# A recurrent scan that steps two head pairs at once

## The chip, the cores and the metric

The kernel runs on one NeuronCore of a Trainium2 chip, in float32 throughout. The metric is the device time of one execution in microseconds (us), taken as the median of several runs. Engines are named as in the profile: PE (TensorE matmul), PEld (its weight loads), DVE (VectorE), ACT (ScalarE), POOL (GpSimd), SP (SyncE, which here only issues DMAs). Each engine takes its instructions in the order in which they were queued.

## The reference

One post-norm layer over 1024 latent tokens with a prefix of 256 context tokens, width 1024. The part that matters here is branch B of the token mixer, a bidirectional RWKV-7 scan with 8 heads of 64 channels:

```python
def delta_scan(state0, inputs, emit):
    def step(S, inp):
        r_t, w_t, k_t, v_t, kk_t, a_t = inp
        s_kk = jnp.einsum('...vk,...k->...v', S, kk_t)
        S = (S * w_t[..., None, :] - s_kk[..., :, None] * (kk_t * a_t)[..., None, :]
             + v_t[..., :, None] * k_t[..., None, :])
        return S, (jnp.einsum('...vk,...k->...v', S, r_t) if emit else None)
    return lax.scan(step, state0, inputs)
...
state_ctx, ys_c = delta_scan(state0, scan_c, ctx_out)   # 256 context tokens, outputs not used
_, ys_l = delta_scan(state_ctx, scan_l, True)           # 1024 latent tokens
```

Around it stand one wide input projection `h @ w_in`, neighbourhood attention (branch A), a chunked gMLP (branch C), the merge of the three branches by gates, and a SwiGLU FFN. Direction 1 of the scan runs over the tokens backwards.

## The kernel before, in words

The program is written as if it ran one stage after the other: projections, scan (`rwkv_run`), 4 projections that only the attention needs, attention with the scan's read-out mixed in, 24 projections that only the merge needs, merge and output projection, FFN. A scheduler then orders the instructions of each engine at build time: what stands earlier in the program has the higher priority, and what is ready and stands later fills the time of an engine that it takes to be idle, as far as tiles and PSUM banks are free. The order is fixed from then on.

The 28 late projections (`filling`, called through `fill`) are the **filler**: each is 48 matmuls of 128 x 128 x 512 (lines 208 to 210, three per product because a float32 is split in a high and a low part), 1344 matmuls in all. They use 2 PSUM banks of their own, tag `d`.

The scan turns the recurrence into products over 64 tokens (a unit). Heads go in pairs: a pair fills 128 partitions. A **job** is one head pair, both directions, and 4 units (256 tokens): 4 pairs x 5 pieces of the sequence = 20 jobs. The list `L` takes the pairs in two groups, and within a group the jobs of its two pairs alternate, so that job m hands its state on to job m+2. For each job there is

- `prep`, per direction: loads of five rows of 256 tokens; exponentials on ACT; products on DVE; the Gram products `ge` and `go` (lines 643, 644) and the transposes `tr` (line 647) into PSUM tiles of tag `gr`; copies from there by DVE (lines 654 to 667, G and others) and ACT (line 670).
- `invert`, for both directions together: the inverse of a unit lower triangular 64 x 64 matrix for each unit and head. G goes out to DRAM (`gs`, line 679) and comes back in another layout (`gz`, line 681); 30 small dependent DVE instructions invert the 16 x 16 diagonal blocks (lines 689 and 691) and one copies the result (line 692); it goes out (`ds`, line 694) and comes back (`Dc`, line 696); `Db` and `Dt` are made of it (line 705); then four rounds of 8 small matmuls each (lines 710 and 719, PSUM tag `ho`), each followed by DVE (lines 712, 722), finish X for one direction, and the same again for the other.
- `step`, for each unit and direction, in the order of the tokens: two products with the state (731, 732), a copy to `ru`, the product with X (736), a negated copy to `ub` by ACT and DVE (740, 741), three products that make the new state and the output (742 to 744), the scaled state (755 by DVE, 756 by ACT) and two copies of the output `y` by ACT (760).

`prepare(m)` (prep and invert) is written two jobs ahead of the steps of job m. Six PSUM banks belong to the scan: three of tag `gr`, one of `ho`, two of `sc` (`ngr` is 3 in line 88). A PSUM tile of a tag waits until one of the tag's banks is free of the tile that had it.

## Time and profile before

| | |
|---|---|
| median of 3 runs | 2478.57 us (2476.95 to 2483.38) |
| the profiled execution | 2475.12 us; its span 2473.3 us |
| granted clock of TensorE | 0.986 on average |
| PE, PEld, DVE, ACT, POOL busy | 96%, 76%, 59%, 33%, 25% of the span |
| scan, from the first Gram product to the last state product | about 517 to 1203 us |
| attention and read-out | about 1203 to 1467 us |
| last filler, then merge, output projection and FFN | 1467 to 1487 us, then to the end |

A row of a group gives how often an instruction ran, its busy time and the mean of one; matmuls are pipelined, so two of them overlap in the records, and the time that one costs PE is read from start to start. Each float32 matmul of the scan is recorded as two passes; a filler matmul is one. A row of the timeline gives start, duration, engine, line and tiles, and in brackets what ended an idle time before it. An SPq or ACTq row is the issue of a DMA on that engine's queue.

### The profile page before, as it was taken

What the parts mean: (1) busy time and instruction counts of PE and PEld (TensorE: products, weight loads), DVE (VectorE), ACT (ScalarE), POOL (GpSimd) and SP (SyncE); (2) the same over time, 40 slices, a digit from 0 to 9 for tenths busy, and PEclk for the clock granted to TensorE, in tenths of its full rate; (3) what the DMA queues carried; (4) which work ended last, traced back from release to release, by engine and by line L of the source; (5) the groups of instructions that cost most, each with busy time, mean ns of one, the idle gap of its engine ahead of it and who ended that gap; (6) DMA issues with size and microseconds to landing.
All of it is one profiled execution on the core that took longest, in us unless ns stands there. A gap on an engine that the chain in (4) does not pass through costs nothing.

```text
span 2473.3 us, 39035 instructions
## 1 busy us (share of the span) xinstructions
PE 2386.2 (96%) x14752; PEld 1879.6 (76%) x14752; DVE 1447.2 (59%) x3318; ACT 819.8 (33%) x1721; POOL 628.3 (25%) x654
## 2 busy tenths in 40 slices
PE   6999999989999999999999999999999999999997
PEld 4778888876777776777777777777778888888886
DVE  8884446357788877887278855685562323232226
ACT  4433334233344433443356632232311121111112
POOL 6220213441112111121132230324522222212224
PEclk9999999999899999999999999999999999999999
DMA  7675434553334433332467656453311111111101
GB/s 253 206 240 159 138 126 164 170 165 78 94 97 108 106 98 94 93 101 62 138 170 204 182 188 233 151 184 118 102 51 52 51 51 43 43 51 47 47 26 69
DMA packets 263840, 293.90 MB, mean 119 GB/s; under 512 B 121666, under 2 KB 192578, under 8 KB 263652
## 3 DMA queue, kind: packets, MB, share of 16 engines
q1 hardware_dynamic: 200852, 213.12, 29.3%
q10 hardware_dynamic: 54608, 51.40, 6.7%
q0 software_dynamic: 8192, 26.88, 2.9%
q8 instruction: 117, 1.92, 0.3%
q14 instruction: 71, 0.58, 0.1%
HBM read 221.06 MB, written 70.26 MB: 118 GB/s over the span
## 4 chain that ended last, share of the span: by engine, by line
PE 65%; DVE 8%; DMA 3%; issue 3%; POOL 2%; ACT 1%; SPq 0%; POOLq 0%; ACTq 0%; DVEq 0%
PE d L209 11%; PE d L208 11%; PE d L210 11%; PE d L1001 3%; PE d L1002 3%; PE d L1000 3%; PE pv L884 2%; PE ho L719 2%; PE gr L644 2%; PE sc L736 2%; PE sc L731 1%; PE gr L643 1%; PE sc L744 1%; PE pt L870 1%; PE sc L742 1%
## 5 line engine op out<-in xcount | busy, mean ns | idle before, releaser
L209 PE MATMUL d<-hl,wh 128*128 128x512 f32 x1584 | 641.6, 405 | 0.4 <-POOL hl L1089 0.4
L208 PE MATMUL d<-hh,wh 128*128 128x512 f32 x1584 | 638.7, 403 | 0.2 <-ACT hh L1086 0.2
L210 PE MATMUL d<-hh,wl 128*128 128x512 f32 x1584 | 636.8, 402 | 0.0
L208 PEld LDWEIGHTS d<-hh,wh 128*128 128x128 f32 x1584 | 299.7, 189 | 64.8 <-issue 1.6
L210 PEld LDWEIGHTS d<-hh,wl 128*128 128x128 f32 x1584 | 299.6, 189 | 64.9 <-issue 2.3
L209 PEld LDWEIGHTS d<-hl,wh 128*128 128x128 f32 x1584 | 299.6, 189 | 61.7 <-POOL hl L1089 1.0
L200 POOL TENSOR_TENSOR wl<-wr,wh 128x256 fp32r<-128x256 f32 (+1 forms) x156 | 192.5, 1257 | 591.2 <-ACT wh L196 536.1
L196 ACT ACTIVATE wh<-wr 128x1024 fp32r<-128x1024 f32 x123 | 130.2, 1059 | 354.3 <-PE d L209 222.7
L1126 DVE TENSOR_TENSOR sl<-sl,d 128x512 f32<-128x512 f32 x44 | 30.2, 687 | 300.9 <-PE d L210 300.9
L200 DVE TENSOR_TENSOR wl<-wr,wh 128x1024 fp32r<-128x1024 f32 x51 | 63.3, 1242 | 160.0 <-ACT wh L196 111.6
L1000 PE MATMUL d<-dwh,S 128*128 128x512 f32 x352 | 137.2, 390 | 2.0 <-DVE acc L1153 2.0
L1001 PE MATMUL d<-dwl,S 128*128 128x512 f32 x352 | 136.9, 389 | 0.0
L1002 PE MATMUL d<-dwh,S 128*128 128x512 f32 x352 | 136.9, 389 | 0.0
L1153 DVE TENSOR_TENSOR acc<-d,acc 128x512 f32<-128x512 f32 x96 | 64.7, 686 | 95.5 <-PE d L1002 95.4
L995 POOL TENSOR_TENSOR dwl<-dr,dwh 128x1024 fp32r<-128x1024 f32 (+1 forms) x24 | 55.5, 2318 | 163.3 <-ACT dwh L994 163.3
L756 ACT ACTIVATE rv<-sc,E 64x64 f32<-64x64 f32 x152 | 46.5, 308 | 139.9 <-DVE rv L755 130.8
L884 PE MATMUL pv<-pT,V 128*64 128x128 f32 (+2 forms) x640 | 92.0, 284 | 0.0
L994 ACT ACTIVATE dwh<-dr 128x1024 fp32r<-128x1024 f32 (+1 forms) x24 | 23.7, 989 | 192.8 <-PE d L1002 185.3
L995 POOL TENSOR_TENSOR wl<-wr,wh 128x1024 fp32r<-128x1024 f32 x16 | 43.7, 2734 | 170.2 <-ACT wh L994 126.5
L225 DVE TENSOR_TENSOR S<-sl,S 128x512 fp32r<-128x512 f32 x44 | 66.2, 1505 | 30.8 <-ACT S L222 30.8
L884 PEld LDWEIGHTS pv<-pT,V 128*64 128x64 f32 (+2 forms) x640 | 69.0, 138 | 16.5 <-issue 11.1
L722 DVE TENSOR_TENSOR X<-ho,Dt 48x192 f32<-48x192 f32 (+2 forms) x240 | 68.3, 285 | 21.5 <-PE ho L719 16.5
(308 smaller groups left out, 4752.8 us busy)
## 6 DMA issues: line engine op xcount, KB each, us to landing
wr<-wgu SPq DMA_DIRECT2D x44, 512.0 KB
wa<-wada SPq DMA_DIRECT2D x32, 512.0 KB
wr<-win SPq DMA_DIRECT2D x31, 512.0 KB
wr<-win ACTq DMA_DIRECT2D x28, 512.0 KB
s_gt<-stg ACTq DMA_DIRECT2D x48, 256.0 KB
wr<-wbr SPq DMA_DIRECT2D x24, 512.0 KB
g<-s_gt SPq DMA_DIRECT2D x48, 256.0 KB
dr<-wdn SPq DMA_DIRECT2D x20, 512.0 KB
```

Of the source, the lines that this page charges most:

```text
L196: nc.scalar.activation(hi[:, :n], raw[:, :n], AF.Copy)
L200: (lo_eng or self.lo_eng).tensor_tensor(lo[:, q], raw[:, q], hi[:, q].bitcast(F32), ALU.subtract)
L208: nc.tensor.matmul(ps, w, xh, start=first and k == 0, stop=False)
L209: nc.tensor.matmul(ps, w, xl, start=False, stop=False)
L210: self.last = nc.tensor.matmul(ps, lo[:, P * k:P * k + P], xh, start=False, stop=last and k == n - 1)
L225: (lo_eng or nc.vector).tensor_tensor(lo, src, hi.bitcast(F32), ALU.subtract)
L722: nc.vector.tensor_tensor(X[z:z + n, :, t0:64], e[z:z + n], Dt[z:z + n, :, t0:64], ALU.add)
L884: nc.tensor.matmul(o, V[0:k, vt, 64 * e:64 * e + 64], pt[0:k, i, :], start=(i == 0), stop=(i == len(cols) - 1))
L995: nc.gpsimd.tensor_tensor(lo[:, 0:512 * n], raw[:, 0:512 * n], hi[:, 0:512 * n].bitcast(F32), ALU.subtract)
L1000: nc.tensor.matmul(ps, xh, wh, start=first, stop=False)
L1001: nc.tensor.matmul(ps, xh, wl, start=False, stop=False)
L1002: nc.tensor.matmul(ps, xl, wh, start=False, stop=last)
```

## The change

A job now holds both head pairs of a group for 128 tokens, 2 units of each pair, so that there are again 20 jobs (2 groups x 10 pieces), with two steps after each other instead of four, and job m hands its state on to job m+1. A step (`step_in`, `step_solve`, `step_out`) takes one unit of both pairs. The copies of a step cover both pairs in one instruction; `ub` and `us` are one form, written by ACT alone; the state is scaled by DVE alone, in one instruction per head. The products of a step stand in two banks, `sa` and `sb` of two buffers each: first and second product in `sa`, state and output in `sb`, there as matmuls of 64 columns, the two column halves one after the other, where before one matmul had 128 columns. That makes 10 matmuls per unit where there were 7 (8 instead of 7 in the context's units). The loads of a job bring two pieces of 128 tokens where they brought one of 256, so there are twice as many DMAs, of half the size; the same holds for the stores of `y`. `gr` has two banks instead of three, and `ho` has none of its own: its tiles are now of tag `gr`.

```diff
@@ -85,7 +85,7 @@
-        self.nd, self.ngr = 2, 3
+        self.nd, self.ngr = 2, 2
...
-            ub = rp.tile([P, P], F32, name=f"ub{i}")
+            ub = rp.tile([P, 2, P], F32, name=f"ub{i}")
             nc.gpsimd.memset(ub, 0.0)
             self.ub.append(ub)
-        L = [(2 * g + j, i) for g in range(2) for i in range(5) for j in range(2)]
+        L = [(g, i) for g in range(2) for i in range(10)]
...
         def values(m):
-            j, i = L[m]
+            g, i = L[m]
             rv = rvs[m] = [[self.T([P, 4, 64], f"rv{d}{h}", 3) for h in range(2)] for d in range(2)]
...
                 for h in range(2):
-                    nc.sync.dma_start(rv[d][h][64 * (1 - h):64 * (1 - h) + 64, 0:4, :],
-                                      bass.AP(V.tensor, V.offset + 64 * h + n0 * P, [[P, 64], [P * 64, 4], [1, 64]]))
+                    for jj in range(2):
+                        V = s["vtok"][2 * g + jj]
+                        nc.sync.dma_start(rv[d][h][64 * (1 - h):64 * (1 - h) + 64, 2 * jj:2 * jj + 2, :],
+                                          bass.AP(V.tensor, V.offset + 64 * h + n0 * P, [[P, 64], [P * 64, 2], [1, 64]]))
...
-        for m, (j, i) in enumerate(L):
+        for m, (g, i) in enumerate(L):
...
-            y = [self.T([P, 2, P], f"y{d}", 2) for d in range(2)] if i else [None, None]
-            for u in range(4):
+            lat = i >= 2
+            y = [self.T([P, 2, P], f"y{d}", 2) for d in range(2)] if lat else [None, None]
+            for uu in range(2):
+                st = [self.step_in(Js[m][d], d, uu, rvs[m][d]) for d in range(2)]
+                ub = [self.step_solve(Js[m][d], *st[d]) for d in range(2)]
                 for d in range(2):
-                    self.step(Js[m][d], d, i, u, rvs[m][d], rvs[m + 2][d] if i < 4 else None, y[d])
-            if i:
+                    self.step_out(Js[m][d], d, uu, ub[d], st[d], rvs[m][d], None if i == 9 else rvs[m + 1][d], y[d])
...
+                    n = i - 2 if d == 0 else 9 - i
+                    for jj in range(2):
+                        nc.scalar.dma_start(s["Y"][d][2 * g + jj][:, P * n:P * n + P], y[d][:, jj, :])
...
     def start(self, d, i):
-        return 0 if i == 0 else (CT + 256 * (i - 1) if d == 0 else NT - 256 * i)
-
-    def prep(self, m, j, d, i):
+        return P * i if d == 0 else (CT - P * (i + 1) if i < 2 else NT - P * (i - 1))
...
-        for t, x in ((li, s["li"][d]), (kk, s["kk"]), (kd, s["kd"][d]), (bb, s["bb"][d])):
-            nc.sync.dma_start(t, x[j][:, n0:n0 + 256])
-        if lat:
-            r = self.T([P, 256], "rl", 2)
-            nc.sync.dma_start(r, s["r"][j][:, n0 - CT:n0 - CT + 256])
+        r = self.T([P, 256], "rl", 2) if lat else None
+        for t, x, n in ((li, s["li"][d], n0), (kk, s["kk"], n0), (kd, s["kd"][d], n0), (bb, s["bb"][d], n0), (r, s["r"], n0 - CT)):
+            for jj in range(2):
+                if t is not None:
+                    nc.sync.dma_start(t[:, P * jj:P * jj + P], x[2 * g + jj][:, n:n + P])
...
         ge = self.ps.tile([P, 4, P], F32, name="gr", tag="gr", bufs=self.ngr)
...
-            e = self.ps.tile([P, 4, 64], F32, name="ho", tag="ho", bufs=1)
+            e = self.ps.tile([P, 4, 64], F32, name="ho", tag="gr", bufs=self.ngr)
...
-                e = self.ps.tile([P, 4, n], F32, name="ho", tag="ho", bufs=1)
+                e = self.ps.tile([P, 4, n], F32, name="ho", tag="gr", bufs=self.ngr)
...
-    def step(self, J, d, i, u, rv, rvn, y):
...
+    def step_in(self, J, d, uu, rv):
         nc = self.nc
+        tt = uu if d == 0 else 1 - uu
+        sa = self.ps.tile([P, 2, 256], F32, name="sa", tag="sa", bufs=2)
+        sb = self.ps.tile([P, 2, 256], F32, name="sb", tag="sb", bufs=2)
+        halves = (slice(0, 64), slice(64, 128))
+        kk = J["KKe"], J["KKo"]
+        for jj in range(2):
+            for z, q in enumerate(halves):
+                nc.tensor.matmul(sa[q, jj, 0:64], kk[z][:, 2 * jj + tt, 0:64], rv[z][:, 2 * jj + tt, :], start=True, stop=True)
+        for jj in range(2):
+            for z in range(2):
+                for h, q in enumerate(halves):
+                    if J["lat"] or h == z:
+                        nc.tensor.matmul(sb[q, jj, 64 * z:64 * z + 64], kk[z][:, 2 * jj + tt, 64 + 64 * h:128 + 64 * h],
+                                         rv[z][:, 2 * jj + tt, :], start=(jj == 0 and (z == 0 or not J["lat"])), stop=False)
+        return tt, sa, sb
+
+    def step_solve(self, J, tt, sa, sb):
+        nc = self.nc
+        ru = self.T([P, 2, 64], "ru", 2)
+        nc.vector.tensor_copy(ru, sa[:, :, 0:64])
+        for jj in range(2):
+            for z in (0, 64):
+                nc.tensor.matmul(sa[z:z + 64, jj, 64:128], J["X"][z:z + 64, 2 * jj + tt, :], ru[z:z + 64, jj, :], start=True, stop=True)
+        self.un += 1
+        ub = self.ub[self.un % 4]
         for z in (0, 64):
+            nc.scalar.activation(ub[z:z + 64, :, z:z + 64], sa[z:z + 64, :, 64:128], AF.Copy, scale=-1.0)
+        return ub
+
+    def step_out(self, J, d, uu, ub, st, rv, rvn, y):
+        nc = self.nc
+        tt, _, sb = st
+        BB, E = J["BB"], J["E"]
+        for jj in range(2):
+            for h in (0, 64):
+                q = slice(h, h + 64)
+                c = slice(0, P) if J["lat"] else q
+                nc.tensor.matmul(sb[q, jj, c], BB[:, 2 * jj + tt, q], ub[:, jj, c], start=False, stop=(jj == 1))
+        if uu == 0 or rvn is not None:
+            n, w = (rv, 1 - tt) if uu == 0 else (rvn, d)
+            for z in range(2):
+                q = slice(64 * z, 64 * z + 64)
+                nc.vector.tensor_tensor(n[z][q, w::2, :], sb[q, :, q], E[q, tt::2, 64:65].to_broadcast([64, 2, 64]), ALU.mult)
+        if J["lat"]:
+            for z, p0 in ((0, 64), (1, 0)):
+                nc.scalar.activation(y[64 * tt:64 * tt + 64, :, 64 * z:64 * z + 64], sb[p0:p0 + 64, :, 64 * z:64 * z + 64], AF.Copy)
```

How this moves instructions on PE, as the built programs have them. First the kernel before, in the middle of the scan. Tiles carry numbers: `ho_7412` belongs to the inversion whose G is `G_7299`, while `gr_8040` to `gr_8095` are the Gram products and transposes of a later job.

```order
L643 MATMUL gr_8040<-KKe4_3962,BK_8035 128x64
L644 MATMUL gr_8041<-KKo4_3963,BK_8035 128x64
...
L647 MATMUL gr_8050<-c_ident_63,BK_8035 128x128 x2
...
L643 MATMUL gr_8085<-KKe5_3966,BK_8080 128x64 x4
L710 MATMUL ho_7412<-Db_7406,G_7299 64x64 x8
L719 MATMUL ho_7423<-Dt_7407,ET_7421 48x48 x8
L719 MATMUL ho_7434<-X_7408,ET_7421 32x32 x8
L644 MATMUL gr_8086<-KKo5_3967,BK_8080 128x64 x4
L719 MATMUL ho_7445<-X_7408,ET_7421 16x16 x8
L647 MATMUL gr_8095<-c_ident_63,BK_8080 128x128 x3
L710 MATMUL ho_7462<-Db_7456,G_7348 64x64 x8
```

The Gram products of a later job stand ahead of and between the rounds of an earlier inversion (filler and step rows, left out here, stand between them).

The same place on PE in the change: the last round of one inversion, the Gram products and transposes of the next job (both directions), and the first round of that same job's inversion (`ho_7084` reads `G_6966`, which is made of `gr_6951` and `gr_6952`).

```order
L724 MATMUL ho_6775<-X_6738,ET_6751 16x16 x7
L648 MATMUL gr_6951<-KKe4_3962,BK_6944 128x128 x3
L649 MATMUL gr_6952<-KKo4_3963,BK_6944 128x128 x3
...
L652 MATMUL gr_6961<-c_ident_63,BK_6944 128x128 x4
...
L648 MATMUL gr_7005<-KKe5_3966,BK_6998 128x128 x4
L649 MATMUL gr_7006<-KKo5_3967,BK_6998 128x128 x4
L652 MATMUL gr_7015<-c_ident_63,BK_6998 128x128 x4
...
L715 MATMUL ho_7084<-Db_7078,G_6966 64x64 x8
```

All Gram products of a job now stand behind the last round of the inversion before it, and this is so for every job of the scan: on PE the order is Gram, transposes, inversion, Gram, transposes, inversion. Between the last transposes and the first round stand 66 filler matmuls and the steps of the job just inverted; around the whole cycle stand some 88 filler matmuls per job (before: 45).

And the place in the change where the filler ends, in the inversion of the 14th of 20 jobs.

```order
L209 MATMUL d_15794<-hl7_597,wh_15759 128x512
L210 MATMUL d_15794<-hh7_596,wl_15760 128x512
L715 MATMUL ho_8964<-Db_8958,G_8846 64x64 x8
L724 MATMUL ho_8975<-Dt_8959,ET_8973 48x48 x8
L724 MATMUL ho_8986<-X_8960,ET_8973 32x32 x8
L724 MATMUL ho_8997<-X_8960,ET_8973 16x16 x8
L715 MATMUL ho_9014<-Db_9008,G_8900 64x64 x8
L755 MATMUL sa_9464<-ru_9492,X_8960 64x64 x4
```

From here on PE has no filler. Of the 1344 filler matmuls 76 stand ahead of the first Gram product and 1268 behind it, up to this place; before it was 72 ahead, 897 up to the end of the scan, and 375 behind it, of which about 140 stand ahead of the first attention score and about 120 behind the last matmul of the read-out.

More of the change, by code (lines that the diff above doesn't have):

```diff
@@ L620, in prep @@
         E = self.T([P, 4, 65], "E", 6)
         nc.gpsimd.memset(E[:, :, 0:1], 1.0)
-        nc.scalar.activation(E[:, :, 1:65], units(R(li)), AF.Exp, scale=-C05)
+        nc.scalar.activation(E[:, :, 1:65], R(li), AF.Exp, scale=-C05)
         le = self.T([P, 256], "le", 2)
-        nc.scalar.activation(le, R(li), AF.Exp, scale=C05)
+        nc.scalar.activation(units(le), R(li), AF.Exp, scale=C05)
         BK = self.T([P, 4, P], "BK", 2)
-        if d:
-            nc.vector.tensor_tensor(BK[:, :, 64:128], units(kd)[:, ::-1, :], units(le)[:, :, ::-1], ALU.mult)
-        else:
-            nc.vector.tensor_tensor(BK[:, :, 64:128], units(kd), units(le), ALU.mult)
@@ L630, in prep @@
-        nc.vector.scalar_tensor_tensor(BK[:, :, 0:64], units(R(bb)), 0.5, units(le), ALU.mult, ALU.mult)
+        nc.vector.tensor_tensor(BK[:, :, 64:128], units(kd), R(le), ALU.mult)
+        nc.vector.scalar_tensor_tensor(BK[:, :, 0:64], R(bb), 0.5, units(le), ALU.mult, ALU.mult)
         KKe, KKo = self.sets[(m % 3) * 2 + d]
-        nc.vector.tensor_tensor(KKe[0:64, :, 0:64], E[0:64, :, 0:64], units(R(kk))[0:64], ALU.mult)
-        nc.vector.tensor_tensor(KKo[64:128, :, 0:64], E[64:128, :, 0:64], units(R(kk))[64:128], ALU.mult)
+        nc.vector.tensor_tensor(KKe[0:64, :, 0:64], E[0:64, :, 0:64], R(kk)[0:64], ALU.mult)
@@ L634, in prep @@
+        nc.vector.tensor_tensor(KKo[64:128, :, 0:64], E[64:128, :, 0:64], R(kk)[64:128], ALU.mult)
         if lat:
-            ee, rr = (E[:, :, 1:65], units(r)) if d == 0 else (E[:, :, 64:0:-1], units(r)[:, ::-1, :])
+            ee, rr = E[:, :, 64:0:-1] if d else E[:, :, 1:65], units(r)
             nc.gpsimd.tensor_tensor(KKe[0:64, :, 128:192], ee[0:64], rr[0:64], ALU.mult)
@@ L724, in invert @@
             J["X"] = X
-    def step(self, J, d, i, u, rv, rvn, y):
+    def step_in(self, J, d, uu, rv):
         nc = self.nc
-        lat, KKe, KKo, BB, X, E = J["lat"], J["KKe"], J["KKo"], J["BB"], J["X"], J["E"]
-        v, w = (u, u + 1) if d == 0 else (3 - u, 2 - u)
-        sc = self.ps.tile([P, 512], F32, name="sc", tag="sc", bufs=2)
-        nc.tensor.matmul(sc[0:64, 0:64], KKe[:, u, 0:64], rv[0][:, v, :], start=True, stop=True)
-        nc.tensor.matmul(sc[64:128, 0:64], KKo[:, u, 0:64], rv[1][:, v, :], start=True, stop=True)
-        ru = self.T([P, 64], "ru", 2)
-        nc.vector.tensor_copy(ru, sc[:, 0:64])
-        for z in (0, 64):
-            nc.tensor.matmul(sc[z:z + 64, 64:128], X[z:z + 64, u, :], ru[z:z + 64], start=True, stop=True)
-        if lat:
-            self.un += 1
-            ub = self.ub[self.un % 4]
-            nc.scalar.activation(ub[0:64, 0:64], sc[0:64, 64:128], AF.Copy, scale=-1.0)
-            nc.vector.tensor_scalar(ub[64:128, 64:128], sc[64:128, 64:128], -1.0, None, ALU.mult)
-            nc.tensor.matmul(sc[:, 128:192], KKe[:, u, 64:192], rv[0][:, v, :], start=True, stop=False)
-            nc.tensor.matmul(sc[:, 192:256], KKo[:, u, 64:192], rv[1][:, v, :], start=False, stop=False)
-            nc.tensor.matmul(sc[:, 128:256], BB[:, u, :], ub, start=False, stop=True)
-            so = 192
-        else:
-            us = self.T([P, 64], "us", 2)
-            nc.scalar.activation(us, sc[:, 64:128], AF.Copy, scale=-1.0)
-            nc.tensor.matmul(sc[0:64, 128:192], KKe[:, u, 64:128], rv[0][:, v, :], start=True, stop=False)
-            nc.tensor.matmul(sc[64:128, 128:192], KKo[:, u, 128:192], rv[1][:, v, :], start=True, stop=False)
-            nc.tensor.matmul(sc[:, 128:192], BB[:, u, :], us, start=False, stop=True)
-            so = 128
-        if not (i == 4 and u == 3):
-            dst = (rv[0][:, w, :], rv[1][:, w, :]) if u < 3 else (rvn[0][:, 3 * d, :], rvn[1][:, 3 * d, :])
-            nc.vector.tensor_scalar(dst[0][0:64], sc[0:64, 128:192], E[0:64, u, 64:65], None, ALU.mult)
-            nc.scalar.activation(dst[1][64:128], sc[64:128, so:so + 64], AF.Copy, scale=E[64:128, u, 64:65])
-        if lat:
-            q = slice(64 * (v % 2), 64 * (v % 2) + 64)
-            for z, p0, c0 in ((0, 64, 128), (1, 0, 192)):
-                nc.scalar.activation(y[q, v // 2, 64 * z:64 * z + 64], sc[p0:p0 + 64, c0:c0 + 64], AF.Copy)
```

18 lines of the change are left out of this document (9 added, 9 removed).

## The prediction

> **What bounds the kernel now.** I read the page first, then busy time by stage, then the timeline of the scan.
>
> ```profile
> span 2473.3 us, 39035 instructions
> PE 2386.2 (96%) x14752; PEld 1879.6 (76%) x14752; DVE 1447.2 (59%) x3318; ACT 819.8 (33%) x1721; POOL 628.3 (25%) x654
> 517.00:1203.00 686.00, 669.50 (x6479) 487.18 (x6479) 519.02 (x1799) 271.83 (x901) 118.87 (x231) 0.97 0.38 97
> 1203.00:1230.00 27.00, 26.61 (x117) 21.50 (x115) 1.49 (x1) 6.99 (x9) 5.69 (x8) 1.00 0.67 200
> 1230.00:1467.00 237.00, 226.89 (x1473) 178.89 (x1474) 188.06 (x576) 128.94 (x245) 63.21 (x39) 0.99 0.62 178
> 1467.00:1487.00 20.00, 20.00 (x89) 16.42 (x88) 3.67 (x5) 5.32 (x8) 3.58 (x6) 1.00 0.93 315
> L208 PE MATMUL d<-hh,wh 128*128 128x512 f32 x300 | 132.4, 441 | 0.0
> ```
>
> The first column of numbers in a stage's row is its length, then come PE, PEld, DVE, ACT and POOL with their counts, then the granted clock. The scan takes 686 us of the 2473.3, the stretches behind it 27, 237 and 20. PE is busy in nearly all of it, but in the scan (last row, one of three lines of the filler) 900 of its matmuls are filler. So PE looks full because something was always at hand to fill it; what sets the pace can be another thing.
>
> ```profile
> 809.36 0.39 PE L210 MATMUL d<-hh,wl 128*128 128x512 f32 x1
> 809.59 0.40 PE L208 MATMUL d<-hh,wh 128*128 128x512 f32 x1
> 809.82 0.39 PE L209 MATMUL d<-hl,wh 128*128 128x512 f32 x1
> L681 SPq DMA_DIRECT2D gz<-gs x20: 573/586/1147, 527.5 to 1145.1; - x20
> L696 SPq DMA_DIRECT2D Dc<-ds x20: 366/374/597, 551.2 to 1166.7; - x20
> ```
>
> A filler matmul costs PE 0.23 us from start to start, so 900 are 207 us, and the scan's own work with its stalls is (686 - 207) / 20 = 24.0 us per job. A new job reaches the load of `gz` every (1145.1 - 527.5) / 19 = 32.5 us. How long is one inversion? The rows of the last job, and of the `ds`, `Dc` of the one before it:
>
> ```profile
> 1138.55 0.36 DVE L692 COPY DD<-DD 64x256 f32<-64x256 f32 x1
> 1138.97 0.59 SPq L694 DMA_DIRECT2D ds<-DD  x1
> 1139.69 0.42 DVE L655 TENSOR_TENSOR G<-gr,c_gmask 64x256 f32<-64x256 f32 x1
> 1142.30 0.38 SPq L696 DMA_DIRECT2D Dc<-ds  x1
> 1142.33 0.58 ACTq L679 DMA_DIRECT2D gs<-G  x1
> 1145.11 0.58 SPq L681 DMA_DIRECT2D gz<-gs  x1
> 1145.37 0.43 DVE L705 TENSOR_TENSOR Db<-Dc,c_bm 128x256 f32<-128x256 f32 x1 [0.70 <-DMA Dc<-ds]
> 1171.32 0.42 DVE L705 TENSOR_TENSOR Db<-Dc,c_bm 128x256 f32<-128x256 f32 x1
> 1173.14 0.42 DVE L712 TENSOR_TENSOR ET<-ho,c_om 128x256 f32<-128x256 f32 x1 [0.46 <-PE ho L710]
> 1180.55 0.43 DVE L712 TENSOR_TENSOR ET<-ho,c_om 128x256 f32<-128x256 f32 x1 [0.82 <-PE ho L710]
> 1185.41 0.47 DVE L722 TENSOR_TENSOR X<-ho,Dt 16x64 f32<-16x64 f32 x2 [0.51 <-PE ho L719]
> ```
>
> G is finished at 1140.1, `Db` starts at 1171.3 (31.2 us later), the last X ends at 1185.9 (14.6 more): 45.8 us from G to X, against a new job every 32.5. **So two inversions overlap**, and they can: while one waits for its DMAs, the three `gr` banks take the Gram products of the next job, and the rounds of the inversion have a bank of their own. The reader should see a latency of 46 us and more per job that is hidden by overlap, and filler poured into its gaps.
>
> **The change, part by part.**
>
> *PSUM banks.* `ho` loses its bank, `gr` one of three. By the order on PE every Gram product of a job now stands behind the last round of the inversion before it, so inversions no longer overlap: the time per job becomes the whole cycle Gram, copies, DMAs, recursion, DMAs, rounds. I add it up from rows. First the copies of the Gram products on DVE:
>
> ```profile
> L655 DVE TENSOR_TENSOR G<-gr,c_gmask 64x256 f32<-64x256 f32 x40 | 16.7, 418 | 3.3 <-PE gr L644 1.9
> L658 DVE TENSOR_TENSOR BB<-gr,c_gmask 64x256 f32<-64x256 f32 x32 | 13.4, 418 | 0.9
> L662 DVE TENSOR_TENSOR KKo<-gr,c_gmask 64x512 f32<-64x512 f32 x32 | 22.2, 693 | 0.9
> L630 DVE SCALAR_TENSOR_TENSOR BK<-bb,le 128x256 f32<-128x256 f32 x40 | 20.1, 502 | 0.3
> L689 DVE TENSOR_TENSOR dtmp<-gz,DD x300: 154/201/785, 534.4 to 1163.4; 64x15 f32<-64x15 f32 x20, 64x39 f32<-64x39 f32 x20, 64x55 f32<-64x55 f32 x20, 64x63 f32<-64x63 f32 x20
> ```
>
> A, Gram to G: direction 0 copies 2 x (0.42 + 0.42 + 0.69) = 3.1 us, two `BK` products of 0.5 follow, direction 1 needs 1.9 more up to its second G (its banks come free only now), and PE's products with the hand-overs take about 2 (an estimate; DVE waits 0.5 to 0.8 for PE in the `ET` rows): 8 us. B, G to `Db`: G to the last `gs` 2.2 (1139.69 + 0.42 to 1142.33; less on an emptier ACT queue, I take 1.9), `gs` to `gz` 2.8, `gz` landing 3.1 (not shown by itself; the like of `Dc`, issued 1142.30 and waited for until 1145.37), the recursion, the copy and the issue of `ds` 0.5, `ds` to `Dc` 3.3, `Dc` landing 3.1, `Db` to the first round 0.6. The recursion is 30 dependent instructions: at least 30 x 0.201 = 6.0 us, and before about 15 (from `gz` landed, 1148.2, to 1163.4) with the steps of other jobs in between; in the change's order of DVE hardly any stand in between, so I take 8.5, near the low end. B is 23.8. C, the rounds: 14.6 before, with filler and step work queued between them; the second direction, with less in its way, took 5.3 from `ET` to its end, so twice that, 10.6, is the low end; I take 12. **The cycle is 8 + 23.8 + 12 = 44 us**, with a low end of 40 (short recursion, rounds at 10.6) and a high end of 50 (recursion at 13, rounds at 14.6).
>
> *The steps.* Twice the work per copy and half the copies take DVE and ACT time off the scan; DVE was busy 519 of 686 us, so this alone sets nothing, but it is why I put the recursion low. The steps of a job now run beside the next inversion and are shorter than it; they cost only at the end. Behind the last X before came 1203 - 1186 = 17 us; with two steps left I take 14 (10 to 17).
>
> *Column halves on PE.*
>
> ```profile
> 807.70 0.22 PE L731 MATMUL sc<-rv,KKe 128*64 128x64 f32 x1
> 807.76 0.22 PE L731 MATMUL sc<-rv,KKe 128*64 128x64 f32 x1
> 808.32 0.40 PE L208 MATMUL d<-hh,wh 128*128 128x512 f32 x1
> 808.64 0.45 PE L736 MATMUL sc<-ru,X 64*64 64x64 f32 x8
> 809.02 0.50 PE L209 MATMUL d<-hl,wh 128*128 128x512 f32 x1
> 810.05 0.33 PE L742 MATMUL sc<-rv,KKe 128*128 128x64 f32 x2
> 810.72 0.33 PE L742 MATMUL sc<-rv,KKe 128*128 128x64 f32 x2
> ```
>
> The state products of a unit cost 0.67 us at full width (810.05 to 810.72). In halves, two matmuls on different column halves run side by side, and a pass of both takes 0.06 (807.70 to 807.76). A unit has six of them, three pairs of two passes, so 0.36, or 0.48 if the products with `ub`, of double width, take 0.12: 8 units save about 2 us per job although there are 10 matmuls for 7. A detour from the filler to small matmuls and back costs (0.32 - 0.23) + (0.38 - 4 x 0.06) = 0.23 beside the work itself; steps of two units make 8 fewer per job, the halves add 4 (the state products used to have the filler's shape): 0.9 less. PE's own work falls from 24 to 21 us per job. [...]
>
> *Filler.* The order puts 88 filler matmuls in each cycle until they are used up in the 14th job. PE then needs 88 x 0.23 + 21 = 41 us per job, just under the cycle of 44: the two fit together and I take the larger. For the last 6 jobs there is no filler, PE stands idle most of the time, and the cycle is 44 less what the filler delays the rounds, 43.
>
> *DMAs.* A job issues about 14 more loads on SP's queue. Before, a load of `kkl` held the queue for 0.33 us:
>
> ```profile
> L615 SPq DMA_DIRECT2D kkl<-s_kk x40: 319/325/584, 491.9 to 1101.0; - x40
> ```
>
> That is 4.6 us more in a cycle of 44; the queue stays mostly empty. Queued behind a load that waits for its buffer are `gz` and `Dc`; two loads of `rl` stand between `ds` and `Dc`, 0.7 us inside the 3.3 that `Dc` waits anyway. Cost nothing; without that cover 0.7 per job.
>
> *Behind the scan.* The 117 filler matmuls of the 27 us row vanish, but not the 27 us:
>
> ```profile
> 1198.92 19.69 SPq L789 DMA_DIRECT2D V<-s_vatok  x16
> L836 PE MATMUL SA<-K,Q x64: 281/386/448, 1230.2 to 1445.3; 128*128 128x264 f32 x16, 128*128 128x352 f32 x16, 128*128 128x288 f32 x16, 128*128 128x384 f32 x16
> ```
>
> The issues of the attention's V alone take SP 19.7 us, and the first score comes at 1230.2 because of them. Inside the 237 us there are some 140 filler matmuls, 33 us; DVE and the chain from block to block hold the rest, so I take 8 (0 to 33). The last 20 us are nothing but filler and go, less about 8 to load the first merge weights that the filler covered: 12. Together 20 less (8 to 40).
>
> *Sum.* Scan: 14 x 44 + 6 x 43 + 14 = 888 us for 686: 202 more. Behind it 20 less. Against the profiled execution (2475.12; the median of the runs is 2478.57, 0.1% off): 2475 + 202 - 20 = **2657 us**. The bounds: 20 x 40 + 14 = 814, with 40 less behind, gives 2563; 20 x 50 + 17 = 1017, with 8 less, gives 2798.
>
> **The rivals.**
>
> *The cycle is the short one*, 40 us, PE's row of filler setting it and everything else fitting: 814, so 2475 + 128 - 20 = 2583. For it: DVE has less to do, and the low rows are real. Against: DMAs and hand-overs at their shortest all at once.
>
> *The cycle is the long one*, 50 us: 1014 for 686, 2783. For it: the last job before, in a scan that was running out, still took 46 from G to X, without A. Against: a good part of that was other jobs' work on DVE.
>
> *The clock drops where the filler is gone.* Before, it dropped where PE had little:
>
> ```profile
> 620.00:630.00 10.00, 9.78 (x118) 6.69 (x116) 9.25 (x31) 4.51 (x12) 2.84 (x4) 1.00 0.45 133
> 630.00:640.00 10.00, 10.00 (x42) 7.36 (x41) 4.07 (x18) 2.60 (x11) 0.00 (x0) 0.53 0.14 45
> ```
>
> 42 matmuls in 10 us and a granted clock of 0.53, 118 and 1.00 just before. The tail has about as few. PE's share of the cycle (an estimate: eight rounds and five groups of Gram products and transposes at about 0.5 as in the row of L736, 6.5 us) would double: 6 x 6.5 = 39 more, 2696. [...]
>
> *Faster, the other side.* If the waits between G and X were nearly all queueing behind other jobs, a cycle alone could be short, and merging would pay on PE. It decides when the scan falls under 686 + 20 = 706 us: 14 jobs of PE at 20.3 + 17 = 37, a cycle no longer than that, and 6 tail jobs of 25: 686, 2455. For it: DVE was three quarters busy. Against: the four DMA legs of the cycle alone (2.8, 3.1, 3.3, 3.1) are 12.3 us, the rounds 10.6, the recursion 6, A 8, so 37 at the very least in the tail.
>
> **How the numbers follow.** Forecast 0.48; clock 0.15; long cycle 0.17; short cycle 0.13; faster 0.05; no change 0.02, by a chance meeting of gains and losses. The range 2590 to 2765 takes in the clock and parts of the two cycles. Slower by over 0.3% (about what a measurement of this kernel can tell from no change): 0.48 + 0.15 + 0.17 + 0.13 = 0.93; within 0.02; faster 0.05.
>
> **What would show it.** Right: `gz` issued every 43 to 45 us; the first round of a job behind its G by 23 to 25 and the next Gram product directly behind the last X; filler up to about 600 us behind the first Gram product and none after; PE busy a third of the tail; the attention as long as before. Wrong: two inversions under way at a time, a step between `gz` issues under 36 us, or PE without idle time to the scan's end.

## The result

The changed kernel takes 2719.8 us (median of 4 runs, 2714.26 to 2731.96), the kernel before 2480.98 us beside it (4 runs): a ratio of 1.0965, 95% interval 1.0937 to 1.0993. It is 239 us slower.

The page of the changed kernel first (its third and fourth row show slices of 68 us, in tenths of PE's busy time and of the granted clock), then busy time by stage, where the columns are length, PE, PEld, DVE, ACT, POOL with counts, granted clock, DMA share and GB/s:

```profile
span 2718.9 us, 40638 instructions
PE 2441.2 (90%) x15584; PEld 1931.0 (71%) x15584; DVE 1441.2 (53%) x3110; ACT 771.8 (28%) x1441; POOL 627.9 (23%) x646
PE   6999999989989899885474899799999999999998
PEclk9999999998898997886766799899999999999999
L715 PE MATMUL ho<-Db,G 64*64 64x64 f32 x640 | 39.8, 291 | 133.2 <-DVE Db L710 133.2
...
517.00:1462.00 945.00, 780.32 (x7685) 589.53 (x7685) 523.34 (x1592) 238.15 (x643) 136.25 (x251) 0.83 0.31 79
1188.00:1424.00 236.00, 141.78 (x1900) 112.90 (x1898) 141.67 (x440) 52.56 (x164) 14.39 (x34) 0.69 0.21 46
...
L208 PE MATMUL d<-hh,wh x422: 387/394/796, 517.8 to 1188.0; 128*128 128x512 f32 x141
```

The scan now takes 945 us where it took 686. DVE is busy for 523 us in it, as before (519). PE is busy for 111 us more, but 1268 filler matmuls run in it instead of 900 (some 85 us), which before stood partly behind the scan. So no engine got more work that would explain 259 us. PE, which had next to no gaps, waits 133 us for `Db` alone, at the first round of each inversion. The filler ends at 1188 us; behind that PE is busy 142 of 236 us, at a clock of 0.69.

The row of the load of `gz`, and one cycle of the part without filler, from the timeline (DVE, ACT's queue, PE and SP's queue):

```profile
L686 SPq DMA_DIRECT2D gz<-gs x20: 573/585/1687, 531.0 to 1423.2; - x20
...
1288.00 0.46 DVE L727 TENSOR_TENSOR X<-ho,Dt 16x64 f32<-16x64 f32 x2 [0.41 <-PE ho L724]
1289.57 0.42 DVE L659 TENSOR_TENSOR G<-gr,c_gmask 64x256 f32<-64x256 f32 x1 [1.10 <-PE gr L648]
1294.73 2.15 ACTq L684 DMA_DIRECT2D gs<-G  x2
1295.85 0.42 DVE L660 TENSOR_TENSOR G<-gr,c_gmask 64x256 f32<-64x256 f32 x1
1298.49 0.58 SPq L686 DMA_DIRECT2D gz<-gs  x1
1302.90 0.17 DVE L694 TENSOR_TENSOR dtmp<-gz,DD 64x15 f32<-64x15 f32 x1
1312.06 0.37 DVE L697 COPY DD<-DD 64x256 f32<-64x256 f32 x1
1314.87 0.37 SPq L701 DMA_DIRECT2D Dc<-ds  x1
1317.86 0.42 DVE L710 TENSOR_TENSOR Db<-Dc,c_bm 128x256 f32<-128x256 f32 x1 [5.43 <-DMA Dc<-ds]
...
1328.61 0.36 PE L724 MATMUL ho<-X,ET 64*16 64x16 f32 x14
1328.90 0.93 PE L648 MATMUL gr<-KKe,BK 64*128 64x128 f32 x6
1329.01 0.47 DVE L727 TENSOR_TENSOR X<-ho,Dt 16x64 f32<-16x64 f32 x2 [0.41 <-PE ho L724]
1330.58 0.42 DVE L659 TENSOR_TENSOR G<-gr,c_gmask 64x256 f32<-64x256 f32 x1 [1.10 <-PE gr L648]
```

Read from X to X this is a closed chain of 41.0 us: the last round, then at once the Gram products of the next job (1328.61, 1328.90), both directions' G, the copies out and in, the recursion, out and in, the rounds. Nothing of the next inversion runs beside it. Over all jobs `gz` is issued every (1423.2 - 531.0) / 19 = 47.0 us, against 32.5 before.

### The profile page after: what moved, and what is told of

Same layout as the page of the kernel before. It is cut to its first block, busy times and chain, and to the rows that moved or that the text cites. A ratio compares the mean times of both kernels' runs of the same rounds, so it can differ in the third digit from the quotient of the medians.

```text
span 2718.9 us, 40638 instructions
## 1 busy us (share of the span) xinstructions
PE 2441.2 (90%) x15584; PEld 1931.0 (71%) x15584; DVE 1441.2 (53%) x3110; ACT 771.8 (28%) x1441; POOL 627.9 (23%) x646
## 5 line engine op out<-in xcount | busy, mean ns | idle before, releaser
L715 PE MATMUL ho<-Db,G 64*64 64x64 f32 x640 | 39.8, 291 | 133.2 <-DVE Db L710 133.2
L715 PEld LDWEIGHTS ho<-Db,G 64*64 64x64 f32 x640 | 32.8, 194 | 140.8 <-DVE Db L710 140.1
L759 ACT ACTIVATE ub<-sa 64x128 f32<-64x128 f32 x160 | 43.5, 272 | 230.1 <-PE sa L755 209.0
```

The lines of the kernel that those rows point to most:

```text
L715: nc.tensor.matmul(e[z:z + 64, u, :], J["G"][z:z + 64, u, :], Db[z:z + 64, u, :], start=True, stop=True)
```

## The experiments

**Is it the banks or the steps?** The theory: shared banks put the inversions one behind the other. The rival: what costs is in the steps (halves, loads of half the size, a state that goes from each job to the very next).

Only the banks of the change, in the kernel before:

```diff
-        self.nd, self.ngr = 2, 3
+        self.nd, self.ngr = 2, 2
...
-            e = self.ps.tile([P, 4, 64], F32, name="ho", tag="ho", bufs=1)
+            e = self.ps.tile([P, 4, 64], F32, name="ho", tag="gr", bufs=self.ngr)
```

(and the same for the `ho` tile of the later rounds.)

> The kernel before with only the PSUM banks changed: gr has 2 banks, and the rounds of the inversion (ho) take them too; steps, jobs, loads and state products as before, so 6 of 8 banks are in use. Bank theory: the Gram products of a job must wait for the last round of the inversion before it, so inversions run one after the other, gz is issued every 44 to 50 us, and the time is 2650 to 2760 us. Rival, that the pace is lost in the steps themselves (matmuls in halves, loads of half the size, state handed on to the next job instead of the one after it): none of these is in this kernel, so it stays at 2475 to 2510 us with gz every 32 to 34 us.

Measured: 2855.56 us, ratio 1.149 (1.1441 to 1.1539). `gz` and the recursion of one of the last jobs:

```profile
L681 SPq DMA_DIRECT2D gz<-gs x20: 574/586/2019, 528.4 to 1533.6; - x20
...
1433.19 0.16 DVE L689 TENSOR_TENSOR dtmp<-gz,DD 64x15 f32<-64x15 f32 x1
1449.37 0.37 DVE L692 COPY DD<-DD 64x256 f32<-64x256 f32 x1
```

A new job every 52.9 us. The banks alone slow the kernel down, by more than the whole change does, and by more than I expected. The rows show where part of the rest lies: with the old steps, ten copies of steps stand between the 30 instructions of the recursion in this job, which takes 16.6 us (1433.19 to 1449.74); in the job of the changed kernel shown above it is one copy and 9.5 us (1302.90 to 1312.43). So in a serial chain everything in the change but the sharing of `gr` and `ho`, taken together, is worth 2855.56 - 2719.8 = 136 us; no run takes the merged copies apart from the rest there. The change as a whole is a gain with a larger loss on top.

Three ways to give the changed kernel its banks back:

```diff
  (1) own bank for ho, three of gr, one buffer each of sa and sb
-        self.nd, self.ngr = 2, 2
+        self.nd, self.ngr = 2, 3
-  name="ho", tag="gr", bufs=self.ngr
+  name="ho", tag="ho", bufs=1
-  name="sa", tag="sa", bufs=2
+  name="sa", tag="sa", bufs=1
-  name="sb", tag="sb", bufs=2
+  name="sb", tag="sb", bufs=1
  (2) own bank for ho, two of gr, one buffer of sb
  (3) three banks that gr and ho share, one buffer of sb
```

> The changed kernel with three gr banks and a bank of its own for ho, paid for by one buffer instead of two for each of sa and sb; all else as changed. Bank theory: two inversions overlap again, gz every 30 to 34 us, 2420 to 2520 us. Rival (steps): the halves, the small loads and the state chain from job to next job are all still there, so it stays above 2650 us with gz every 44 us or more.

> The changed kernel with a bank of its own for ho, two gr banks as changed, and one buffer for sb. Bank theory in the form that sharing is what hurts: the Gram products of the next job can pass the rounds, so inversions overlap although gr has only two banks: gz every 31 to 37 us, 2430 to 2560 us. In the form that the number of gr banks hurts: 2600 us or more.

> The changed kernel with three banks that gr and ho share (one buffer for sb). Bank theory, sharing hurts: the tiles take the shared banks in the order of the program, Gram products behind the rounds, so gz is still issued every 43 to 48 us and the time is 2640 to 2740 us; the number of banks adds little. If the number hurts: 2580 us or less.

The scan is taken from the first Gram product to the end of the last state product; by that measure it is 688 us in the kernel before.

| | banks | us | ratio to the kernel before | scan us | `gz` every |
|---|---|---|---|---|---|
| changed | 2 shared | 2719.8 | 1.0965 (1.0937 to 1.0993) | 946 | 47.0 |
| (1) | 3 + own | 2423.84 | 0.9747 (0.9717 to 0.9777) | 616 | 29.1 |
| (2) | 2 + own | 2461.71 | 0.9895 (0.9879 to 0.9910) | 626 | 29.6 |
| (3) | 3 shared | 2722.36 | 1.0953 (1.0931 to 1.0975) | 950 | 47.2 |

The rows for (1), (2) and (3) in this order, with the scan's row of (1) and three rows of its timeline:

```profile
L686 SPq DMA_DIRECT2D gz<-gs x20: 573/582/1535, 531.1 to 1083.4; - x20
...
517.00:1133.00 616.00, 574.10 (x7240) 417.47 (x7242) 489.05 (x1593) 219.24 (x616) 115.92 (x220) 0.97 0.44 106
...
886.67 0.41 DVE L659 TENSOR_TENSOR G<-gr,c_gmask 64x256 f32<-64x256 f32 x1
890.64 0.47 DVE L727 TENSOR_TENSOR X<-ho,Dt 16x64 f32<-16x64 f32 x2 [0.31 <-PE ho L724]
...
898.56 0.47 DVE L727 TENSOR_TENSOR X<-ho,Dt 16x64 f32<-16x64 f32 x2
```

```profile
L686 SPq DMA_DIRECT2D gz<-gs x20: 573/580/1639, 533.9 to 1096.7; - x20
```

```profile
L686 SPq DMA_DIRECT2D gz<-gs x20: 573/580/730, 529.3 to 1425.7; - x20
```

In (1) the first G of a job is copied (886.67) while the X of the job two ahead of it are still to come (890.64, 898.56) and the job between is in its recursion: the inversions overlap again. All of the 239 us come back, and 63 more. The split between (2) and (3) tells which property of the banks it is; the two differ in nothing else, three banks for `gr` and `ho` in each. Two Gram banks are enough if the rounds have their own (2462 us); three are no use if the rounds share them (2722 us). Tiles of one tag take its banks in the order of the program, so with two banks all 40 recorded Gram products and transposes of a job stand behind the last round of the job before it on PE. With three, 2 of the 40 come ahead of the rest of that last round (at 876.78 us in (3), 0.7 us ahead of it), and 38 still stand behind it. So with two or three banks it is the sharing that counts, not the number; more than three were not tried. Two groups of products in one rotation were then not independent of each other (2722 us, against 2462 with a bank apart).

Version (1) is faster than both kernels, by 2.5% and 10.9%.

**Column halves.** One bank for all products of a step, two banks in all, `gr` and `ho` as before the change; the state products stand behind the product with X (they share its bank now). Once with halves, and once with the state products of the latent units at full width:

```diff
-        sa = self.ps.tile([P, 2, 256], F32, name="sa", tag="sa", bufs=2)
-        sb = self.ps.tile([P, 2, 256], F32, name="sb", tag="sb", bufs=2)
+        sc = self.ps.tile([P, 2, 256], F32, name="sc", tag="sc", bufs=2)
...
  (full width, besides)
+                if J["lat"]:
+                    nc.tensor.matmul(sb[:, jj, 64 * z:64 * z + 64], kk[z][:, 2 * jj + tt, 64:192],
+                                     rv[z][:, 2 * jj + tt, :], start=(jj == 0 and z == 0), stop=False)
...
+                nc.tensor.matmul(sb[:, jj, 0:P], BB[:, 2 * jj + tt, :], ub[:, jj, :], start=False, stop=(jj == 1))
```

> The changed kernel with three gr banks, a bank of its own for ho, and all products of a step in one bank (two banks in all, one for each direction, as before the change); the state products are issued behind the product with X instead of ahead of it. Bank theory: jobs overlap as in the run with own banks and one buffer each (2424 us there), and the two directions no longer share step banks, so the same or a little better: 2390 to 2430 us, gz every 28 to 30 us. Rival, that the state products ahead of the X product (not the banks) brought part of the gain there: 2430 to 2480 us.

> As the run before it (one bank per step), but the state products of the latent units at full width: 3 matmuls of 128 columns per unit instead of 6 of 64 columns. My estimate of the halves (2 us per job on PE, 0.9 more by fewer detours from the filler, less 4 detours for the halves): at full width 16 jobs lose some 2 us each where PE is full, so 10 to 45 us slower than the run before it. Rival, that the change of tiling costs more than the halves save: at full width as fast or up to 30 us faster.

Measured: halves 2443.28 us, ratio 0.9834 (0.981 to 0.9857); full width 2440.07 us, 0.9813 (0.9785 to 0.9841). The intervals overlap widely: the halves bring nothing that can be measured in the whole. In the scan they bring a little. One of three lines of the filler and the scan's row for version (1), for halves in one bank, and for full width:

```profile
L208 PE MATMUL d<-hh,wh x272: 387/397/775, 519.4 to 1133.8; 128*128 128x512 f32 x136
```

```profile
L208 PE MATMUL d<-hh,wh x256: 387/397/793, 516.0 to 1124.9; 128*128 128x512 f32 x128
516.00:1124.00 608.00, 564.89 (x7194) 409.38 (x7194) 492.81 (x1593) 216.43 (x612) 115.28 (x216) 0.97 0.43 106
```

```profile
L208 PE MATMUL d<-hh,wh x269: 387/397/796, 520.5 to 1145.7; 128*128 128x512 f32 x135
518.00:1145.00 627.00, 593.48 (x6466) 447.98 (x6466) 488.28 (x1593) 218.30 (x615) 118.24 (x220) 0.97 0.43 104
```

With 0.23 us per filler matmul, the scan's own time on PE, stalls included, is 608 - 768 x 0.23 = 431 us with halves and 627 - 807 x 0.23 = 441 at full width: 0.5 us per job. That is the net saving, with the detours that the halves add; the prediction's figures give 2 - 4 x 0.23 = 1.1 for the same, and the expectation 2. What the halves save there is not seen at the end: the full width takes the side of its rival, as fast or faster. Its scan is 19 us longer and the rest 19 us shorter; about half of each is filler that moved into the scan, the rest of what comes back behind it is open. Version (1) has 616 - 816 x 0.23 = 428, the kernel before 688 - 897 x 0.23 = 482: 2.7 us less per job, of which the halves are about 0.5 and the rest of the new steps the remainder. The run with halves, 2443 us against the 2424 of version (1), lies in the range of its rival, that state products ahead of the X product are worth something. In the profiled executions (2440.3 against 2428.8) its scan is 8 us shorter than that of (1) and the part behind it some 20 longer. It has 48 filler matmuls fewer in its scan, and they then run behind it: 11 of the 20 us. The rest is open.

**Filler or clock?** The first cycles of the changed kernel are near 48 us, the last ones 42 on average, and the last ones are those at a low clock. All filler is held back until the scan has ended, in both kernels:

```diff
         self.rwkv_run()
-        self.fill(4)
         cm_r.__exit__(None, None, None)
+        cm_lw, self.wrp = self.pool("late", side="left")
+        self.fill(28)
+        cm_lw.__exit__(None, None, None)
```

> The changed kernel with all filler held back until the scan is over (its weight tiles take memory that the scan gives free); same work. Filler theory: what made the first cycles 47 us and the last 42 was filler queued between the rounds; so now every cycle is 41 to 43 us from the start, the scan takes 850 to 880 us (945 changed), the granted clock in it is low (0.5 to 0.7), and the time is 2830 to 2930 us, since some 280 us of filler come behind the scan and about 90 are saved in it. Clock theory: the low clock slows the rounds, so the cycles are 46 us or more all along and the scan takes 930 us or more.

> The kernel before with all filler held back until the scan is over; same work. If the scan before was set by PE with its filler, it gets shorter than 686 us: DVE was busy 519 us of it and PE's own work 479, so 540 to 620 us, and the time is 2480 + 207 less 65 to 150, 2540 to 2620 us. If it was set by the latency of the overlapped inversions, it stays at 660 to 690 us, and the time is 2640 to 2690 us.

Changed kernel: 2895.28 us in one run, scan 846 us, `gz` every 42.0 us. Kernel before: 2831.64 us in one run, scan 792 us. The first is as the filler theory had it, with the scan just under the expected range: over the cycles from the end of X of the first job to that of the 14th the mean is 42.4 us where the changed kernel has 48.4, and many are 41, although the clock is lower (0.67 in the scan). A stretch of the changed kernel with filler shows how (the DVE rows are of one job in the middle of the scan, to be set beside 1317.86 to 1329.48 above; the PE rows of the job two later):

```profile
900.23 0.42 DVE L710 TENSOR_TENSOR Db<-Dc,c_bm 128x256 f32<-128x256 f32 x1 [6.16 <-DMA Dc<-ds]
908.50 0.42 DVE L717 TENSOR_TENSOR ET<-ho,c_om 128x256 f32<-128x256 f32 x1 [0.15 <-PE ho L715]
914.46 0.47 DVE L727 TENSOR_TENSOR X<-ho,Dt 16x64 f32<-16x64 f32 x2 [0.42 <-PE ho L724]
...
989.73 0.39 PE L209 MATMUL d<-hl,wh 128*128 128x512 f32 x1
991.02 0.68 PE L715 MATMUL ho<-Db,G 64*64 64x64 f32 x16 [0.91 <-DVE Db L710]
991.64 0.50 PE L210 MATMUL d<-hh,wl 128*128 128x512 f32 x1
...
992.53 0.56 PE L724 MATMUL ho<-Dt,ET 64*48 64x48 f32 x16
```

Filler stands between the rounds in the order of PE, and the rounds take 14.7 us (900.23 to 914.93) where they take 11.6 without. So filler that hides latency while inversions overlap lengthens the chain once they don't.

The two theories were set against each other, but the clock has a part in this. In the second to the 13th job 16 or 17 filler matmuls stand among the rounds each time. The rounds take 12.4 us in the one job whose rounds ran at a clock of 1.00, 13.9 to 14.7 in the five at 0.88, and 16.4 to 17.8 in the six at 0.62 to 0.69. The rounds of the 11th and of the tenth job, from `Db` to the last X:

```profile
1040.60:1058.40 17.80, 17.21 (x182) 11.62 (x183) 6.66 (x21) 1.90 (x5) 0.25 (x1) 0.62 0.15 48
990.50:1003.00 12.50, 11.97 (x179) 8.31 (x180) 6.99 (x22) 2.75 (x8) 0.11 (x1) 1.00 0.15 56
```

Without filler they take 11.6 to 11.9 us at 0.50 to 0.59. So at the low clock the filler among them adds some 5 to 6 us; at the full clock the rounds with filler are hardly longer than that.

The second result met neither expectation: the kernel before got slower in its scan when work was taken out of it. Its windows, and for the changed kernel without filler four of 4.1 us from one cycle:

```profile
510.00:1303.00 793.00, 681.26 (x5600) 549.17 (x5600) 498.97 (x1802) 233.70 (x844) 63.92 (x166) 0.50 0.26 59
```

```profile
743.40:747.50 4.10, 0.00 (x0) 0.00 (x0) 3.59 (x16) 0.00 (x0) 0.41 (x1) 0.82 0.61 147
...
755.70:759.80 4.10, 2.00 (x32) 1.65 (x32) 2.12 (x6) 0.75 (x2) 0.00 (x0) 0.50 0.01 1
...
763.90:768.00 4.10, 4.10 (x70) 3.39 (x67) 2.56 (x9) 0.76 (x3) 0.00 (x0) 0.68 0.00 0
768.00:772.10 4.10, 3.04 (x48) 2.67 (x46) 2.88 (x7) 1.09 (x4) 0.00 (x0) 1.00 0.17 36
```

In that cycle of the changed kernel the clock is 1.00 in the Gram and step products, falls to 0.50 while PE waits for the recursion and the DMAs, and is still 0.50 in most of the rounds. In the kernel before it is 0.50 on average over the whole scan, with PE busy 681 of 793 us.

**What is the low clock worth, and what lifts it?** Products that nobody reads are added to the kernels without filler: on `gz`, 10 for each job in both kernels and then 30 in the changed one; and in the kernel before 20 of the filler's form for each job.

```diff
  (on gz; WARM is 10 or 30)
+            pw = self.dps()
+            for q in range(WARM):
+                nc.tensor.matmul(pw[:, 0:256], c["ident"][0:64, :], z.rearrange("p a b -> p (a b)"), start=True, stop=True)
  (of the filler's form)
+        for q in range(20):
+            nc.tensor.matmul(pw, hh[:, 0:P], hh[:, 0:512], start=True, stop=True)
+        nc.vector.tensor_tensor(pz, pw[0:64, 0:16], z[:, 0, :], ALU.mult)
```

> The changed kernel with all filler held back until the scan is over, as in the run above it, and 10 products of 64 x 128 x 256 for each job that nobody reads, on the loaded gz; on PE they stand ahead of the rounds, in time in which PE had nothing to do. Clock theory: without them the rounds ran at a granted clock of 0.50 and took 11.6 us from Db to X; with PE busy up to a few us ahead of them they run at 0.8 to 1.0 and take 9 to 10.5 us, the cycle falls from 41.0 to 38.5 to 40 us, and the scan from 846 to 800 to 830 us. Rival: the rounds are hand-overs between PE and DVE, the clock sets nothing: cycle 40.5 to 41.5 us and scan 838 to 855 us, or longer if the products are still under way when Db is ready.

> The kernel before with all filler held back until the scan is over (scan 792 us at a granted clock of 0.50, PE busy 88% of it) and the same 10 products per job that nobody reads. Clock theory: that scan was PE at half clock, and the clock stayed down because PE was never busy without a break; 20 x 10 more products fill breaks, the clock goes up in a good part of the scan, and with more work it gets shorter: 680 to 770 us. Rival, that the scan without filler is long for its order of instructions and not for the clock: the added products cost 20 x 7 to 15 us or hide, the clock stays near 0.5, and the scan takes 790 us or more.

> As the run with 10 idle products per job, but with 30: there 10 took 4.6 us, were done 10 us ahead of the rounds, and the rounds again ran at 0.50; 30 should take 13.7 us and end about 1 us ahead of them. Clock theory: now the rounds run at 0.8 to 1.0 and take 9 to 10.5 us from Db to X instead of 11.6, the cycle falls from 41.0 to 38.5 to 40 us, and the scan from 846 to 800 to 830 us. Rival, rounds are hand-overs: cycle 40.5 to 41.5 us in spite of the higher clock.

> The kernel before with all filler held back until the scan is over, and for each job 20 products that nobody reads, of the filler's form (128 x 128 x 512 on the rounded half of the input); a small product with gz ends each row. The run with 10 small products per job left the clock at 0.50 with PE busy 96%. Clock theory: products of the filler's form raise the granted clock to 0.9 or more, and with 20 x 20 x 0.23 = 92 us of added work the scan gets shorter than without any (792 us): 660 to 740 us. Rival, order and not clock: the clock stays near 0.5 or the scan takes 790 us or more.

Changed kernel, 10 products: 2921.99 us (2 runs), scan 871 us. They were done 10 us ahead of the rounds, which ran at 0.50 again, with many cycles at 41.0: the run does not tell the theories apart. With 30: 3026.39 us (one run), scan 978 us, far outside what either theory expected, and two kinds of cycles. In half of the jobs the products ran at 0.50 and held up the rounds by 9 to 13 us, and the cycle is 50 to 58 us. In the others the clock was up when they began, and the rounds came on time: in five the clock had fallen again by then, in the other five it was still up (0.92 to 1.00 from `ET` to `ET`). One of these five, clock and timeline, and a job of the kernel without filler and without added products:

```profile
1258.00:1262.00 4.00, 1.99 (x51) 1.64 (x50) 2.17 (x7) 0.76 (x2) 0.00 (x0) 1.00 0.24 22
1262.00:1266.00 4.00, 2.94 (x72) 2.44 (x72) 2.03 (x7) 0.54 (x2) 0.00 (x0) 0.91 0.02 4
...
1260.60 0.42 DVE L725 TENSOR_TENSOR ET<-ho,c_om 128x256 f32<-128x256 f32 x1
1264.83 0.42 DVE L725 TENSOR_TENSOR ET<-ho,c_om 128x256 f32<-128x256 f32 x1 [0.16 <-PE ho L723]
```

```profile
1260.69 0.42 DVE L719 TENSOR_TENSOR ET<-ho,c_om 128x256 f32<-128x256 f32 x1 [0.55 <-PE ho L717]
1265.77 0.42 DVE L719 TENSOR_TENSOR ET<-ho,c_om 128x256 f32<-128x256 f32 x1 [0.59 <-PE ho L717]
```

From one `ET` to the next, a direction's rounds take 4.23 us at full clock and 5.08 at half. The 4.23 is the same in all four jobs at 1.00, and the 5.08 in 19 of the 20 jobs of the kernel without filler, all at 0.50. So without filler the low clock costs about 0.85 us per direction, or 1.7 per cycle if both directions are alike; in the job shown all rounds together took 10.5 us for 11.6.

Kernel before, 10 products: 2958.0 us (2 runs), scan 909 us. PE was busy 861 of 910 us and the clock was 0.51. The step of the theory that a busier PE lifts the clock has fallen. With products of the filler's form: 2855.59 us (one run), scan 813 us at a clock of 0.63.

```profile
510.00:1420.00 910.00, 861.06 (x5984) 650.24 (x5982) 496.56 (x1797) 233.04 (x844) 61.58 (x154) 0.51 0.22 52
```

```profile
510.00:1325.00 815.00, 739.50 (x5947) 562.32 (x5946) 498.90 (x1819) 233.45 (x844) 64.49 (x157) 0.63 0.25 58
```

By the letter that is the rival's side too (over 790 us). But 400 products that would take 92 us at 0.23 added only 20 to the scan and 58 to PE's busy time, so the rest of PE's work got cheaper as the clock rose from 0.50 to 0.63 (a record of the product of `ub` and `BB` is 409 ns long on average from 560 to 1260 us, where it was 474). How much of the 792 us is the clock, and how much another order of the instructions, is not settled.

## Why the prediction was right, and where it was off

- **The main step held.** The prediction said that Gram products stand behind the last round and that inversions no longer overlap. The rows at 1328.61 and 1328.90 show it, and the runs with the banks show that it costs more than the whole loss: 2424 us without it, 2856 with it alone. The rest of the change, taken together, is a gain.
- **The term that was mis-sized is the cycle with filler: 44 us predicted, 48.4 measured** ((1202.0 - 572.6) / 13, from the end of X of the first job to that of the 14th). The working took the larger of the chain (44) and PE's row (41). They are not side by side, though: filler stands in PE's order between the rounds, so the rounds took 14.7 us (the median as well), not 12. With the same filler they took 12.4 in the job at full clock; the prediction priced its filler at the full clock, and its clock rival came only where the filler is gone. The recursion took 10.4 (median of those jobs) with copies of steps between its instructions, not 8.5. The first two jobs of the second head group took 55 each, with 10 us from the first G to the last and 7 from `gs` to `gz`; I had no term for them. In the scan's ledger: first job 56, 13 cycles 629, last six 252, end 8, together 946 before rounding, where the prediction had 14 x 44 = 616, 258 and 14, 888. Its own sign, `gz` every 43 to 45 us, failed too: 47.0; and the filler lasted some 670 us behind the first Gram product, not 600.
- **The cycle without filler was right**: 43 predicted, 42.1 measured ((1454.4 - 1202.0) / 6). In the cycle shown, A was 7.8 us for 8, B 22.1 for 23.8 (`gs` went out at once where 1.9 were predicted, and the recursion took 9.5 for 8.5), C 11.6 for 12. There is some luck in it: the 1.7 us of the low clock are in the measured cycle and not in the predicted one, and the shorter legs make up for them.
- **PE idle in the tail**: "busy a third of the tail" was wrong. It was busy 60% (142 of 236 us), in part because the same products take longer at the low clock (a direction's first round is 1.12 us long on PE at 1318.34, at 0.50, and 0.68 at 991.02, at 1.00).
- **The clock rival** was right that the clock falls where the filler is gone (0.69 in the tail, 0.50 in most of the rounds) and wrong in its price there: 6.5 us per cycle predicted, about 1.7 measured. Most of a round is then hand-over that does not follow the clock: from `ET` to `ET` it is 4.23 us at 1.00 and 5.08 at 0.50. Its evidence was misread: in the row from 630 to 640 PE is busy 10.00 of 10 us, and 9.78 of 10 in the row before it. The matmuls are few there because each takes longer at 0.53 (the record of a filler matmul is 0.79 us long at 632, at a clock of 0.50, and 0.39 at 809, at 1.00), not because PE had little to do. Where the clock cost more, up to 5 us in a job's rounds, was in the cycles with filler.
- **Steps.** "PE's own work falls from 24 to 21 us per job" came out at 21.4 in version (1), where it can be read. Its parts were off: net of the detours that they add, the halves saved 0.5 instead of 1.1, and the rest of the new steps 2.2 instead of 1.8. The relief of DVE and ACT, of which the prediction said that it "alone sets nothing", was worth more in the serial chain than it saw, since the recursion is part of the chain. With all else in the change but that sharing it makes up the 136 us between the two serial kernels. No run shows what it is worth alone.
- **Small loads on SP's queue** cost nothing that shows: version (1) has them all and is the fastest. A small cost hidden in its gain is not excluded.
- **Behind the scan** 15 us were gained for 20 predicted; that it came so near is partly luck. The first score came 17 us behind the last state product and not 28, while the 16 issues of V took 10.5 us where they took 19.7:

```profile
1459.20 10.46 SPq L807 DMA_DIRECT2D V<-s_vatok  x16
```

The attention was 9 us longer (233.9 for 224.5) where 8 less were predicted, and the part behind it 13 shorter, as predicted (12). Why the issues got faster was not tested, but in the traces it goes with the filler. In the three kernels whose filler was used up before the scan's end (the changed one, version (3), and the kernel before with the banks alone) they took 10.2 to 11.4 us. In the five where filler still ran then (the kernel before, versions (1) and (2), and the two with one bank per step) they took 19.1 to 19.9.

So 2657 missed 2720 by 63 us: 58 in the scan, nearly all of it in the cycles with filler, and 5 behind it. The first job took 12 more than a cycle of the forecast, and the last six jobs and the end 12 less, which cancel. The rival of a cycle of 50 us had the better size for the first 14 jobs, the forecast for the last six.

## What to carry to other kernels

Before two kinds of tile share PSUM banks, ask whether one kind belongs to the next round of a latency chain: in one rotation it waited here for the end of this round, and one more bank did not help (2722 us with three shared, 2462 with two and one apart). A full PE row proves little when it is filled from elsewhere: look for the period at which new work enters, and compare it with the latency of one piece. And when a change is slow, undo its parts one by one: here all but the banks was a gain of 2.5%, in version (1), that the banks hid.

## What the runs showed of the hardware that I had not expected

- Taking the filler out of the scan of the kernel before made that scan longer, 792 us for 688, at a granted clock of 0.50. A busy PE is not enough for the full clock here: with PE busy 95% of 910 us the clock was 0.51, while the changed kernel without filler averaged 0.67 with PE busy 477 of 846 us, and came back to 1.00. In the cycle shown PE works again from the window at 755.7 (2.00 of 4.1 us, at 0.50), is busy throughout from 763.9 (4.10 us, at 0.68), and has 1.00 from the window at 768 on. The kernel before without filler averaged 0.50 over 793 us, with PE busy 681 of them. What differs between the two is the kind of products (column halves in the one, full width in the other) and the breaks between them; which of these counts was not tried.
- The same 16 DMA issues took 19.7 us of SP's time in one kernel and 10.5 in the other, the shorter time in those kernels whose filler was through by then.
- The same 16 or 17 filler matmuls among the rounds of an inversion made the rounds 12.4 us long at a granted clock of 1.00 and up to 17.8 at 0.62.
